# A two-layer hybrid backbone: the experts' activations kept in PSUM, and the gates' two parts summed by TensorE

## The chip, the cores and the metric

The kernel runs on one core of one Trainium2 chip. The metric is the device time of one execution in microseconds: three runs of the kernel before took 4037.82, 4032.03 and 4036.75 us, median 4036.75.

## The reference

Two layers over 256 latent and 256 context tokens of width 1024. Layer 0 mixes by a short gated convolution beside grouped attention, layer 1 by a bidirectional RWKV-7 recurrence. After the mixer of each layer stands a PEER expert network; the change is inside it:

```
def chunk_fn(xc):
    q = (xc @ w_q).reshape(n, PEER_HEADS, 2, PEER_HALF)
    s = jnp.einsum('nhpd,hpkd->nhpk', q, sub_keys)
    s1, i1 = lax.top_k(s[:, :, 0], PEER_TOPK)
    s2, i2 = lax.top_k(s[:, :, 1], PEER_TOPK)
    ...
    top_s, pos = lax.top_k(cand_s, PEER_TOPK)
    idx = jnp.take_along_axis(cand_i, pos, axis=-1)
    gate = jax.nn.softmax(top_s, axis=-1)
    act = jax.nn.gelu(jnp.einsum('nd,nhkd->nhk', xc, u_tab[idx]), approximate=False)
    return jnp.einsum('nhk,nhkd->nd', gate * act, v_tab[idx])
```

There are 128 x 128 = 16384 experts of one neuron each. Every token takes 16 of them for each of 8 heads.

## The kernel before

The kernel doesn't gather experts. It computes all 16384 activations for 256 tokens densely, 128 experts at a time, and multiplies them by a gate matrix that is zero for experts not chosen. One such group of 128 experts is called an expert tile here, numbered E. There are three passes of 128 tiles: the context tokens of layer 0 (E 0 to 127), its latent tokens (E 128 to 255), both in one `Peer` object, and, in a second object after layer 1's mixer, the latent tokens of layer 1.

Float32 precision comes from splits: a value is cast to `fp32r` on ScalarE (`S.copy` in `split`, L1175) and the remainder is subtracted on VectorE or GpSimd (L1176). A product of two split operands is three TensorE products (`mm3`, L1180 to L1182).

For each tile, `Peer.run` issues:

- `first(E)`: 24 products of 128 x 256 into `H`, a bank of PSUM, then Gelu on ScalarE into `W` in SBUF (L1056);
- `gate(E)`: VectorE multiplies `W` by the gates `G` of that tile into `W2` in SBUF (L1062), ScalarE casts it to `gwh`, VectorE subtracts to get `gwl`;
- every second tile, `gen(gq, j)`: the gates of 16 tokens for the quarter `gq` of 32 tiles that comes next. VectorE builds one-hot matrices `oh`, `eq` and `A` (a high and a low part of the gate) in fp16, TensorE multiplies them (L1007) into two PSUM tiles with both parts side by side, ScalarE copies the high part into `G` (L1011) and VectorE adds the low part (L1012). Only for quarter 0 of each object does TensorE accumulate both parts in one tile (L1000), which ScalarE copies whole (L1001);
- `last(E - 1)`: the second product of the tile before, 12 products of 128 x 512 (L1077) into four PSUM accumulators `acc`, then the split of the next `v` (cast on ScalarE, subtraction on GpSimd) and its load on the SP queue;
- the split of the next `u` (the subtraction half on VectorE, half on GpSimd, L1037) and its load.

Tiles 0 to 31 of each object (`LOOK`) have `first` done beforehand, while the experts are still being chosen, and keep their 32 results `W0` to `W31` in SBUF; in the loop they run only gate and second product.

From tile 32 to 255 the first object carries other work between its own, the shadow: choosing the experts of the latent tokens (to tile 92), layer 1's modulation (93 to 124) and layer 1's recurrence over the context tokens (132 to 253; 8 groups of two heads, 4 scan steps each). `beside` hands it out: each tile has four slots, and a task moves on when the units done fall behind a straight line from its start to its end. The tile planner then fixes each engine's order at compile time.

PSUM has eight banks, four for tiles tagged `acc`, which the accumulators of a pass occupy, and four for those tagged `mm`: `H`, the gates' tiles `p` and all products of the shadow take these in turn. In a scan step they are `rhs` (L469, L473), `pu` (L478) and `pS` (L488).

Of the kernel before, what the change touches and what calls it, by code (L numbers as in the profile page):

```python
# [7 lines left out]
F32 = mybir.dt.float32  # L8
# [4 lines left out]
AF = mybir.ActivationFunctionType  # L13
# [48 lines left out]
NSEL, NADA, NCTX = 68.0 + 16 * WKEYS + 16 * WPAIR, 30.0, 326.0 + 69 * WPROJ  # L62
TSEL, TCTX = 92, 132
LOOK = 32
WB = 4
GSCALE = 32768.0


# [122 lines left out]
def do(gen):  # L191

    while True:
        try:
            next(gen)
        except StopIteration as e:
            return e.value
# [22 lines left out]
def beside(work, at):  # L220


    done, slot = [0.0] * len(work), [at]

    def shadow(E):
        at = slot[0]
        slot[0] += 1
        for i, (t0, t1, n, gen) in enumerate(work):
            due = n * (at - 4 * t0) / (4 * (t1 - t0))
            while at > 4 * t0 and (done[i] < due or at >= 4 * t1):  # L230
                try:
                    done[i] += took(next(gen))
                except StopIteration:
                    break

    return shadow
# [588 lines left out]
class Peer:  # L825
# [6 lines left out]
    def __init__(self, k, keep, passes, shadow=None, h=None):  # L832
        self.k, self.keep, self.passes, self.shadow, self.h = k, keep, passes, shadow, h
        self.NT = 128 * len(passes)
        self.XS, self.IT, self.ACC, self.GT, self.U, self.V, self.W = {}, {}, {}, {}, {}, {}, {}
        self.es = ExitStack()
# [135 lines left out]
    def gen(self, gq, j):  # L972

        n, q = divmod(gq, 4)
        pl, V = self.pl, self.k.V
        i16, g16 = self.IT[n]
        if j == 0:
            self.GT[gq] = self.pg[gq % 2].tile([128, 32, 256], F32, name="G")
        s = slice(16 * j, 16 * j + 16)

        def per_token(t):

            return t[:, s].rearrange("p (t u) -> p t u", u=2)[:, :, None, :]


        oh = self.po.tile([128, 8, 128, 2], F16, name="oh")
        V.tensor_tensor(oh, self.iotaR[:, None].to_broadcast([128, 8, 128, 2]), per_token(i16[:, 1]).to_broadcast([128, 8, 128, 2]), ALU.is_equal)  # L987
        sh = [128, 8, 32, 2]
        A = pl.tile([128, 2, 8, 32, 2], F16, name="A", bufs=1)
        eq = pl.tile([128, 8, 32, 2], F16, name="eq", bufs=1)  # L990
        V.tensor_tensor(eq, self.iotaR[:, None, 32 * q:32 * q + 32].to_broadcast(sh), per_token(i16[:, 0]).to_broadcast(sh), ALU.is_equal)
        for i in range(2):
            V.tensor_tensor(A[:, i], eq, per_token(g16[:, i]).to_broadcast(sh), ALU.mult)  # L993
        G = self.GT[gq]
        if gq == 0:
            p = self.k.acc()
            for m in range(16):
                t, u = divmod(m, 2)
                for i in range(2):
                    self.k.T.matmul(p[:, 32 * m:32 * m + 32], lhsT=oh[:, t, :, u], rhs=A[:, i, t, :, u], start=i == 0, stop=i == 1)  # L1000
            self.k.S.copy(G[:, :, s].rearrange("p e n -> p n e"), p.rearrange("p (n e) -> p n e", n=16))  # L1001
            return
        for h in range(2):
            p = self.k.mm()
            for m in range(8):
                t, u = divmod(8 * h + m, 2)
                self.k.T.matmul(p[:, 64 * m:64 * m + 64], lhsT=oh[:, t, :, u], rhs=A[:, :, t, :, u], start=True, stop=True)  # L1007
            t = 16 * j + 8 * h
            p4 = p.rearrange("p (n i e) -> p n i e", n=8, i=2)
            g = G[:, :, t:t + 8].rearrange("p e n -> p n e")  # L1010
            self.k.S.copy(g, p4[:, :, 0])  # L1011
            V.tensor_tensor(g, g, p4[:, :, 1], ALU.add)  # L1012
# [33 lines left out]

    def first(self, E, slot=lambda: None):
        n = E // 128
        H = self.k.mm()
        u, x = self.U.pop(E), self.XS[n]  # L1050
        for t in range(8):
            self.k.mm3(H[:, :256], (u[0][:, t], u[1][:, t]), (x[0][:, t], x[1][:, t]), t == 0, t == 7)
            if t == 3:
                slot()
        W = self.pw.tile([128, 256], F32, name=f"W{E}") if E < LOOK else self.pl.tile([128, 256], F32, name="W", bufs=WB)
        self.k.S.activation(W, H[:, :256], AF.Gelu)  # L1056
        self.W[E] = W

    def gate(self, E):
        pl = self.pl  # L1060
        W2 = pl.tile([128, 256], F32, name="W2", bufs=1)
        self.k.V.tensor_mul(W2, self.W[E], self.GT[E // 32][:, E % 32])  # L1062
        wh = pl.tile([128, 256], F32R, name="gwh", bufs=2)
        wl = pl.tile([128, 256], F32R, name="gwl", bufs=2)
        self.k.split(wh, wl, W2)
        self.W[E] = (wh, wl)

    def second(self, E, slot=lambda: None):
        n, e = divmod(E, 128)
        if e == 0:  # L1070
            self.ACC[n] = [self.k.acc(name=f"acc{i}") for i in range(4)]
        wh, wl = self.W.pop(E)
        vh, vl = self.V.pop(E)
# [65 lines left out]
class K:  # L1139
# [454 lines left out]
    def out_proj(self, ws, pl, ch, cl, gate, h):  # L1594

        for g in range(4):
            wh, wl = next(ws)
            gt = self.gate_cols(pl, gate[0], 2, gate[1], 256 * g, 256)
            for b in range(2):
                p = self.mm()  # L1600
                s = slice(128 * b, 128 * b + 128)
                for k in range(8):
                    self.mm3(p[:, :256], (ch[:, k, s], cl[:, k, s]), (wh[:, k], wl[:, k]), k == 0, k == 7)
                y = pl.tile([128, 256], F32, name="yproj", bufs=2)
                cs = slice(256 * g, 256 * g + 256)
                self.V.tensor_mul(y, p[:, :256], gt)
                self.P.tensor_tensor(h[:, b, cs], h[:, b, cs], y, ALU.add)
            yield
# [591 lines left out]
```

## Time and profile before

| | |
|---|---|
| median of three runs | 4036.75 us (4032.03 to 4037.82) |
| the profiled execution | 4039.33 us, span 4037.5 us, mean granted clock 0.925 |
| busy, share of the span | PE 87%, DVE 77%, POOL 50%, ACT 43% |
| on the chain that ended last | PE 32%, DVE 18%, issue 3%, POOL 2%, ACT 1% of the span |

Busy is the time in which an engine worked; PE is TensorE, DVE is VectorE, ACT is ScalarE, POOL is GpSimd, and PEld is TensorE's loading of weights beside its products. The chain is followed back from the last instruction to what released each; the shares of the chain add up to 56%, as it reaches back to 1736 us only. The two `Peer` loops lie at 490 to 2630 us and 3325 to 4030 us of the span.

### The profile page before, as it was taken

Reading aid. Unit: us, or ns where it says so; the run is one execution under the profiler, and the core shown is the slowest. Engines: PE = TensorE matmul, PEld = TensorE weight load, DVE = VectorE, ACT = ScalarE, POOL = GpSimd, SP = SyncE. Lnnn points to the kernel's source line nnn. Section 1 sums busy time; section 2 is a strip of 40 time slices with the busy share of each in tenths; the row PEclk is TensorE's granted clock in tenths of the full one; section 3 lists DMA queues with packets and bytes.
Section 4 is the critical chain, followed back from the end, with each engine's and each line's share of the span. In section 5 each row is a group of like instructions: output and inputs, shape, how many; then the busy total and the mean of one; then the engine's idle time right before and its main releaser. Section 6 shows DMA issues by size and latency. Waiting matters only on the chain.

```text
span 4037.5 us, 69764 instructions
## 1 busy us (share of the span) xinstructions
PE 3528.5 (87%) x27239; PEld 3038.3 (75%) x27239; DVE 3115.6 (77%) x5626; ACT 1734.0 (43%) x2929; POOL 2024.0 (50%) x1126
## 2 busy tenths in 40 slices
PE   7998878997899989988888889987778787999999
PEld 6687757986778878866677677776666775898898
DVE  3559898779976788687777776577786979999944
ACT  3343444544444444544343343343313344455544
POOL 2022545654556555644444444544435353577776
PEclk9999899998999989988898999987788899999999
DMA  7462345654478745543333333451014234555565
GB/s 231 130 226 90 105 126 167 190 175 126 132 243 262 234 138 168 168 121 101 100 111 106 101 128 114 136 157 52 22 49 137 74 116 125 156 177 174 178 189 156
DMA packets 298644, 574.23 MB, mean 142 GB/s; under 512 B 36901, under 2 KB 193449, under 8 KB 297289
## 3 DMA queue, kind: packets, MB, share of 16 engines
q1 hardware_dynamic: 298312, 569.77, 45.8%
q8 instruction: 213, 3.49, 0.4%
q14 instruction: 119, 0.97, 0.1%
HBM read 555.51 MB, written 14.19 MB: 141 GB/s over the span
## 4 chain that ended last, share of the span: by engine, by line
PE 32%; DVE 18%; issue 3%; POOL 2%; ACT 1%; DMA 0%; DVEq 0%; POOLq 0%; ACTq 0%
PE acc L1077 11%; PE mm L1180 5%; PE mm L1181 5%; PE mm L1182 5%; DVE prod L437 2%; DVE gwl L1176 2%; DVE TT L440 2%; DVE A L993 1%; DVE oh L987 1%; DVE ul L1037 1%; PE mm L806 1%; DVE G L1012 1%; PE mm L669 1%; DVE t L661 1%; PE mm L1007 1%
## 5 line engine op out<-in xcount | busy, mean ns | idle before, releaser
L1176 POOL TENSOR_TENSOR vl<-raw,vh 128x1024 fp32r<-128x1024 f32 x352 | 912.3, 2592 | 755.5 <-ACT vh L1175 631.5
L1037 POOL TENSOR_TENSOR ul<-raw,uh 128x512 fp32r<-128x512 f32 x448 | 714.6, 1602 | 548.1 <-ACT uh L1034 499.1
L1180 PE MATMUL mm<-xh,uh 128*128 128x256 f32 x3072 | 905.8, 295 | 25.2 <-ACT uh L1034 24.4
L1181 PE MATMUL mm<-xh,ul 128*128 128x256 f32 x3072 | 896.2, 292 | 7.6 <-POOL ul L1037 3.9
L1182 PE MATMUL mm<-xl,uh 128*128 128x256 f32 x3072 | 890.6, 290 | 0.0
L1180 PEld LDWEIGHTS mm<-xh,uh 128*128 128x128 f32 x3072 | 609.4, 198 | 50.4 <-ACT uh L1034 25.2
L1181 PEld LDWEIGHTS mm<-xh,ul 128*128 128x128 f32 x3072 | 610.1, 199 | 22.6 <-POOL ul L1037 6.7
L1182 PEld LDWEIGHTS mm<-xl,uh 128*128 128x128 f32 x3072 | 609.7, 198 | 19.6 <-issue 18.2
L1077 PE MATMUL acc<-vh,gwh 128*128 128x512 f32 x1536 | 530.9, 427 | 98.6 <-ACT gwh L1175 98.1
L1077 PE MATMUL acc<-vh,gwl 128*128 128x512 f32 x1536 | 520.2, 420 | 77.9 <-DVE gwl L1176 77.5
L1062 DVE TENSOR_TENSOR W<-W,G 128x256 f32<-128x256 f32 x384 | 312.8, 815 | 356.5 <-ACT W L1056 354.9
L1077 PE MATMUL acc<-vl,gwh 128*128 128x512 f32 x1536 | 507.7, 412 | 0.8 <-DVE vl L1176 0.8
L1175 ACT CAST vh<-raw 128x1024 fp32r<-128x1024 f32 x384 | 404.0, 1052 | 143.8 <-issue 70.5
L1077 PEld LDWEIGHTS acc<-vh,gwl 128*128 128x128 f32 x1536 | 294.9, 199 | 183.8 <-DVE gwl L1176 125.6
L1175 ACT CAST gwh<-W 128x256 fp32r<-128x256 f32 x384 | 155.9, 406 | 640.4 <-DVE W L1062 569.5
L1034 ACT CAST uh<-raw 128x1024 fp32r<-128x1024 f32 x384 | 400.5, 1043 | 35.0 <-DMA raw<-in_peer_u_dram 34.8
L1077 PEld LDWEIGHTS acc<-vh,gwh 128*128 128x128 f32 x1536 | 274.2, 199 | 160.0 <-ACT gwh L1175 114.8
L1056 ACT ACTIVATE W<-mm 128x256 f32<-128x256 f32 x384 | 147.1, 383 | 499.1 <-PE mm L1182 496.3
L1077 PEld LDWEIGHTS acc<-vl,gwh 128*128 128x128 f32 x1536 | 304.0, 199 | 73.6 <-DVE vl L1176 1.7
L987 DVE TENSOR_TENSOR oh<-iotaR,i 128x2048 f16<-128x2048 f16 x192 | 336.1, 1751 | 20.7 <-ACT i L902 20.6
L1176 DVE TENSOR_TENSOR gwl<-W,gwh 128x256 fp32r<-128x256 f32 x384 | 328.1, 855 | 10.7 <-ACT gwh L1175 10.2
L1037 DVE TENSOR_TENSOR ul<-raw,uh 128x512 fp32r<-128x512 f32 x320 | 272.2, 851 | 44.2 <-ACT uh L1034 40.4
(418 smaller groups left out, 6297.9 us busy)
## 6 DMA issues: line engine op xcount, KB each, us to landing
raw<-in_peer_u_dram SPq DMA_DIRECT2D x384, 512.0 KB, 3.7
raw<-in_peer_v_dram SPq DMA_DIRECT2D x384, 512.0 KB, 3.7
wraw<-in_ada_w_dram SPq DMA_DIRECT2D x48, 1024.0 KB, 6.7
wraw<-in_peer_wq_dram SPq DMA_DIRECT2D x16, 1024.0 KB, 9.0
wraw<-in_ev_w_in_dram SPq DMA_DIRECT2D x9, 1024.0 KB
wraw<-in_ev_w_out_dram SPq DMA_DIRECT2D x8, 1024.0 KB, 8.1
wraw<-in_peer_wq_dram SPq DMA_DIRECT2D x16, 512.0 KB
wraw<-in_od_w_k_dram SPq DMA_DIRECT2D x8, 512.0 KB, 5.5
```

Of the source, the lines that this page charges most:

```text
L437: e.tensor_tensor(pv, TT[:, :, 0:c, t, None].to_broadcast(sh), L[:, t + 1:, :, t].rearrange("p t g -> p g t")[:, :, None, :].to_broadcast( ...
L987: V.tensor_tensor(oh, self.iotaR[:, None].to_broadcast([128, 8, 128, 2]), per_token(i16[:, 1]).to_broadcast([128, 8, 128, 2]), ALU.is_equal)
L1034: k.S.copy(uh, ur)
L1037: (le or (k.V, k.P)[i]).tensor_sub(ul[:, t], ur[:, t], uh[:, t].bitcast(F32))
L1056: self.k.S.activation(W, H[:, :256], AF.Gelu)
L1062: self.k.V.tensor_mul(W2, self.W[E], self.GT[E // 32][:, E % 32])
L1077: self.k.T.matmul(self.ACC[n][2 * tb + dh], lhsT=a[:, 128 * tb:128 * tb + 128], rhs=b[:, 512 * dh:512 * dh + 512], start=e == 0 and a is w ...
L1175: self.last_copy = self.S.copy(hi, src).ins
L1176: (le or self.V).tensor_sub(lo, src, hi.bitcast(F32))
L1180: self.T.matmul(out, lhsT=ah, rhs=bh, start=start, stop=False)
L1181: self.T.matmul(out, lhsT=al, rhs=bh, start=False, stop=False)
L1182: self.T.matmul(out, lhsT=ah, rhs=bl, start=False, stop=stop)
```

## The change

The list of buffers for `W` goes. In `first`, the result of tiles from 32 on is no longer copied to SBUF: Gelu writes it back into its own PSUM bank `H`. In `gate` the product with the gates is written into the same bank, or, for the first 32 tiles, whose `W` is still in SBUF, into a fresh `mm` bank. The split reads from there. In `gen`, the accumulating form that only quarter 0 had is used in all quarters of the object that has a shadow (the first two passes), in an `mm` bank but for quarter 0; the third pass keeps the two tiles and the additions for its quarters 1 to 3.

```
@@ gen
-        if gq == 0:
-            p = self.k.acc()
+        if gq == 0 or self.shadow:
+            p = self.k.mm() if gq else self.k.acc()
             for m in range(16):
                 t, u = divmod(m, 2)
                 for i in range(2):
                     self.k.T.matmul(p[:, 32 * m:32 * m + 32], lhsT=oh[:, t, :, u], rhs=A[:, i, t, :, u], start=i == 0, stop=i == 1)
             self.k.S.copy(G[:, :, s].rearrange("p e n -> p n e"), p.rearrange("p (n e) -> p n e", n=16))
             return
@@ first
-        H = self.k.mm()
+        H = self.k.mm()[:, :256]
...
-        W = self.pw.tile([128, 256], F32, name=f"W{E}") if E < LOOK else self.pl.tile([128, 256], F32, name="W", bufs=WB)
-        self.k.S.activation(W, H[:, :256], AF.Gelu)
+        W = self.pw.tile([128, 256], F32, name=f"W{E}") if E < LOOK else H
+        self.k.S.activation(W, H, AF.Gelu)
@@ gate
-        W2 = pl.tile([128, 256], F32, name="W2", bufs=1)
-        self.k.V.tensor_mul(W2, self.W[E], self.GT[E // 32][:, E % 32])
+        W = self.W[E]
+        W2 = self.k.mm()[:, :256] if E < LOOK else W
+        self.k.V.tensor_mul(W2, W, self.GT[E // 32][:, E % 32])
         wh = pl.tile([128, 256], F32R, name="gwh", bufs=2)
         wl = pl.tile([128, 256], F32R, name="gwl", bufs=2)
         self.k.split(wh, wl, W2)
```

## Rows read from the trace of the kernel before

**Rows 1.** Busy time by stage: stretch, length, engines, clock, DMA share, GB/s.

```profile
490.00:640.00 150.00, 118.72 (x772) 89.08 (x771) 141.62 (x189) 67.17 (x107) 65.89 (x23) 0.94 0.42 128
640.00:1127.00 487.00, 439.00 (x3101) 391.55 (x3100) 418.49 (x927) 228.16 (x360) 276.10 (x132) 0.95 0.53 160
1127.00:1423.00 296.00, 282.00 (x2188) 233.54 (x2187) 212.39 (x278) 140.72 (x235) 173.41 (x82) 0.97 0.76 249
1423.00:2630.00 1207.00, 1050.18 (x7951) 886.47 (x7950) 899.77 (x1445) 506.13 (x901) 603.35 (x347) 0.91 0.41 123
3325.00:3468.00 143.00, 113.32 (x666) 85.08 (x665) 134.84 (x180) 62.07 (x100) 55.24 (x19) 0.92 0.40 125
3468.00:4030.00 562.00, 562.00 (x3958) 506.47 (x3956) 431.21 (x474) 283.55 (x445) 406.86 (x191) 1.00 0.58 176
```

**Rows 2.** Groups by line: busy us, mean ns of one, idle before and releasers.

```profile
L1176 DVE TENSOR_TENSOR gwl<-W,gwh 128x256 fp32r<-128x256 f32 x384 | 328.1, 855 | 10.7 <-ACT gwh L1175 10.2
L1062 DVE TENSOR_TENSOR W<-W,G 128x256 f32<-128x256 f32 x384 | 312.8, 815 | 356.5 <-ACT W L1056 354.9
```

**Rows 3.** Single instructions, by tile and by line: ns least/median/most, first and last start.

```profile
L1062 DVE TENSOR_TENSOR W<-W,G x384: 354/425/2608, 499.5 to 4025.2; 128x256 f32<-128x256 f32 x192
...
L1176 DVE TENSOR_TENSOR gwl<-W,gwh x384: 373/420/3552, 502.5 to 4026.1; 128x256 fp32r<-128x256 f32 x192
...
L682 DVE TENSOR_TENSOR R<-mm,r x24: 677/691/692, 1801.8 to 2553.7; 128x512 f32<-128x512 f32 x24
...
L1037 DVE TENSOR_TENSOR ul<-raw,uh x320: 650/684/2887, 503.7 to 4014.8; 128x512 fp32r<-128x512 f32 x160
```

**Rows 4.** Timeline at 3520 and 3527 us: start us, duration us, engine, line, operation.

```profile
3520.59 2.60 POOL L1176 TENSOR_TENSOR vl<-raw,vh 128x1024 fp32r<-128x1024 f32 x1 [1.22 <-DVE ul L1037]
...
3520.84 1.35 DVE L1012 TENSOR_TENSOR G<-G,mm 128x256 f32<-128x256 f32 x2
...
3527.51 2.40 POOL L1176 TENSOR_TENSOR vl<-raw,vh 128x1024 fp32r<-128x1024 f32 x1 [2.08 <-ACT vh L1175]
...
3527.74 2.45 DVE L1062 TENSOR_TENSOR W<-W,G 128x256 f32<-128x256 f32 x1 [0.76 <-ACT W L1056]
```

**Rows 5.** Timeline of VectorE, one round of two tiles among the first 32.

```profile
549.75 1.37 DVE L1012 TENSOR_TENSOR G<-G,mm 128x256 f32<-128x256 f32 x2
...
558.31 1.36 DVE L1012 TENSOR_TENSOR G<-G,mm 128x256 f32<-128x256 f32 x2
```

**Rows 6.** Timeline of TensorE: the accumulating burst of quarter 0, and the other.

```profile
3257.46 0.97 PE L1000 MATMUL acc<-A,oh 128*128 128x32 f16 x32
...
3527.10 0.66 PE L1007 MATMUL mm<-A,oh 128*128 128x64 f16 x16
```

**Rows 7.** Waits of TensorE in 490 to 2630: us in total, times, longest.

```profile
PE acc L1077 <- ACT gwh L1175: 94.1, 54, 4.7
PE acc L1077 <- DVE gwl L1176: 58.2, 55, 4.9
```

**Rows 8.** The chain of waits in 1736 to 2630, by line, shares of the stretch.

```profile
by line: PE acc L1077 13.1%; PE mm L1180 7.2%; PE mm L1182 6.2%; PE mm L1181 6.1%; DVE prod L437 5.7%; DVE TT L440 5.5%; DVE gwl L1176 4.9%; DVE ul L1037 4.4%; issue 4.2%; DVE oh L987 3.4%; PE mm L669 3.4%; DVE G L1012 2.9%; DVE t L661 2.7%
```

**Rows 9.** Timelines of TensorE, ScalarE and VectorE around one scan step.

```profile
2060.01 0.39 PE L1180 MATMUL mm<-xh,uh 128*128 128x256 f32 x1
...
2064.43 0.33 PE L478 MATMUL mm<-rsb,R 64*64 64x64 f32 x4
...
2066.56 0.66 PE L1007 MATMUL mm<-A,oh 128*128 128x64 f16 x16
...
2068.61 0.45 PE L488 MATMUL mm<-UV,tok 128*64 128x64 f32 x6
...
2070.14 0.39 PE L1180 MATMUL mm<-xh,uh 128*128 128x256 f32 x1
...
2067.61 0.39 ACT L1056 ACTIVATE W<-mm 128x256 f32<-128x256 f32 x1
...
2071.13 3.55 DVE L1176 TENSOR_TENSOR gwl<-W,gwh 128x256 fp32r<-128x256 f32 x1
```

More of the change, by code (lines that the diff above doesn't have):

```diff
@@ L64 @@
 LOOK = 32
-WB = 4
 GSCALE = 32768.0
@@ L1048, in first @@
         n = E // 128
-        H = self.k.mm()
+        H = self.k.mm()[:, :256]
         u, x = self.U.pop(E), self.XS[n]
         for t in range(8):
-            self.k.mm3(H[:, :256], (u[0][:, t], u[1][:, t]), (x[0][:, t], x[1][:, t]), t == 0, t == 7)
+            self.k.mm3(H, (u[0][:, t], u[1][:, t]), (x[0][:, t], x[1][:, t]), t == 0, t == 7)
             if t == 3:
                 slot()
-        W = self.pw.tile([128, 256], F32, name=f"W{E}") if E < LOOK else self.pl.tile([128, 256], F32, name="W", bufs=WB)
-        self.k.S.activation(W, H[:, :256], AF.Gelu)
+        W = self.pw.tile([128, 256], F32, name=f"W{E}") if E < LOOK else H
+        self.k.S.activation(W, H, AF.Gelu)
         self.W[E] = W
```

## The prediction

> **What bounds the kernel now.** I read the busy times by stage first, then the chain of waits, then what TensorE waits for, then single instructions. By stage [rows 1] the reader sees three regimes. The last 562 us (third pass from expert 32 on) have TensorE busy for all of it at granted clock 1.00: nothing done on VectorE can help there. The two stretches of 150 and 143 us in which experts 0 to 31 are only summed (their first product was made earlier) are VectorE's: 141.62 and 134.84 us busy, TensorE 118.72 and 113.32. Between them, 640 to 2630, both are near their limit: TensorE 90% busy in 640 to 1127, 95% in 1127 to 1423, 87% in 1423 to 2630, at clocks from 0.91 to 0.97, VectorE 72 to 86%. The chain of 1736 to 2630 [rows 8] mixes TensorE's products with VectorE's lines, so of a microsecond taken from either, the other gives part back. TensorE waits in 490 to 2630 most for the gate's two results, 94.1 and 58.2 us [rows 7].
>
> VectorE's lines are long for a reason that the rows show. The gate's product takes 425 ns in the median but 815 in the mean and 2608 at most, `gwl` 420, 855 and 3552 [rows 2, 3]. At 3527.74 the product starts 0.23 us after a GpSimd subtraction of 2.40 us and ends 0.28 us after it; at 3520.84 two additions that read one operand from PSUM run through under a GpSimd subtraction, 1.35 us for both [rows 4]. So a VectorE operation with both inputs in SBUF is held by a running GpSimd one, and one with a PSUM input is not.
>
> **The change part by part.** The sums are made against the profiled execution, 4039.33 us (span 4037.5 and 1.83 around it); it lies 2.58 us above the median 4036.75, and the forecast is carried over to the median.
>
> *Additions of the low part.* The gates of the second to eighth quarter (7 x 16 = 112 calls) lose two VectorE additions each, 1.35 to 1.37 us a pair [rows 4, 5]. Sixteen of them lie in 490 to 640: there one round of two experts lasts 549.75 to 558.31, 8.56 us, filled by VectorE [rows 5]. 16 x 1.35 = 21.6; I take -20, since TensorE follows at 118.72/150 of 8.56, 6.8 us a round. Of the other 96 calls, 30 lie in 640 to 1127, 20 in 1127 to 1423, 46 in 1423 to 2630 (none after expert 223). The chain gives the additions 2.9% of 894 us = 26 us [rows 8], where 32 calls last 43 us: 60% on the path. 76 x 1.35 x 0.6 = 61; the 20 calls beside a TensorE at 95% I count as nothing. Half of the 61 stays, because TensorE is late next: -30 (ends 0 and -61).
>
> *The gate's operations are held less.* From expert 32 on the product reads PSUM and SBUF, and `gwl` too in all passes; before expert 32 the product still reads two SBUF tiles. The excess is 815 - 425 = 390 and 855 - 420 = 435 ns each. On the chain `gwl` has 4.9% of 894 = 44 us [rows 8], of it 435/855 = 51%, 22 us; for the other 800 us of shadowed work (487, and 1423 to 1736) in proportion 20. The first rounds of passes one and three add little, their product stays held. The wait then meets the next operation with two SBUF inputs (`oh` or `A`), so I keep 60%: -25 (ends 0 and -42). In the last 562 us it is worth 0: TensorE hides it.
>
> *Cost of PSUM operands on VectorE and ScalarE.* VectorE's reading: 691 ns for 512 elements from PSUM against 684 from SBUF [rows 3], so 0. [...] VectorE writing to PSUM, and ScalarE writing it in place, the trace does not show. Between 354 ns (the fastest product) and 691 (twice the elements) [rows 3] I take the median 425, being the nearest row, hence no cost; the upper end is 266 ns x 256 = 68 us of VectorE, half on the path, +34. ScalarE reads the same 256 columns from PSUM in 0.39 us already [rows 9]; the cast from there I cost at nothing, ScalarE, 42 to 48% busy in these stages [rows 1], covering it. The one wide ScalarE copy of the gates replaces two half ones over the same elements, also nothing.
>
> *TensorE's accumulation.* 16 products of 64 columns become 32 of 32. The trace has both: 0.66 us a burst, and 0.97 [rows 6]; +0.31 x 112 = 35 us. In the first 16 VectorE hides them. The 20 calls in 1127 to 1423 count whole, 6; of the other 76 (24 us) half: +18 in all (ends +6 and +30). Nothing new waits for POOL, SP or a transfer; no DMA is moved.
>
> *PSUM banks held longer.* `H` was free after Gelu; it now stays until `gwl`. At one scan step: first product of `H` 2060.01, Gelu done at 2068.0, `gwl` done at 2074.68 [rows 9], so 8.0 us become 14.7. There are four `mm` banks; behind `H` come the scan's `pu`, the gates' `p` and the scan's `pS` [rows 9], and the next expert's `H` (2070.14) is the fifth: it would wait 4.5 us, or, if `gwl` is no longer held (2071.13 + 0.42), 1.4. Behind it on TensorE stand its 24 products, the rest of the scan step and the second product, and the scan's chain waits for those. Such steps number 8 x 4 = 32: 45 to 144 us of TensorE time. In 640 to 1423 fewer products of the shadowed work lie between, and the one `p` instead of two eases it; in the third pass only `p`, `p` and one `H` lie between: 0. I take the low price and a third of it on the path: +15 (ends 0 and +144).
>
> *Clock.* Fewer gate waits leave TensorE less idle; it runs at 0.91 to 0.97 where it waits and at 1.00 where it doesn't [rows 1]. One part in a hundred of 1990 us is 20; I take -12 (ends 0 and -40).
>
> Sum: -20 - 30 - 25 + 0 + 18 + 15 - 12 = -54. 4039.33 - 54 = 3985.3; at the median 4036.75 - 54 = 3983. The instructions' order on each engine is fixed at compile time and is not that of the source (`A` of a call runs beside another expert's gate), so all of it will be laid anew; my ends are wide for that.
>
> **The rivals.**
>
> *A. VectorE was the whole limit.* What is late next is not TensorE but nothing: the additions give 20 + 61, the port 42, the clock 40, TensorE costs 18: -145, 3892. For it: the gate waits of 152 us [rows 7] and VectorE at 94% in the first stage. Against: TensorE 87 to 95% busy between.
>
> *B. TensorE takes all of it back.* Between 640 and 2630 the relief ends at TensorE, which has 35 us more to do: -20 - 25 + 35 + 15 = +5, 4042. For it: 95% in 1127 to 1423. Against: 13% idle in 1423 to 2630.
>
> *C. The held banks serialize the scan (slower).* If each of the 32 scan steps waits the full 4.5 us on the path, +144 against -69 of the other terms: +75, 4112. It decides from 69/32 = 2.2 us a step. For it: `gwl` comes 7 us after Gelu in the rows, because VectorE is behind. Against: 1.4 us once `gwl` isn't held. [...]
>
> *D. PSUM operands cost VectorE more than the rows at 512 elements.* [...]
>
> **How the numbers follow.** Less than 0.2% (8 us) cannot be told from no change. Forecast 0.48, its own range 3930 to 4025; A 0.14; D 0.06; B 0.11; C 0.21. Faster: 0.48 + 0.14 + 0.06 = 0.68. Same 0.10, slower 0.22 (B's upper part and C). The range 3895 to 4065 leaves out the better half of A (0.07) and the greater part of C (0.13).
>
> **What would show it.** Right: the additions gone from 490 to 2630; `gwl`'s mean near 0.45 us in all passes, the product's too but in the first 32 experts; 112 bursts of 0.97 us; a first stage shorter by 20 us; the last 562 us unchanged; less waiting for `gwh` and `gwl`. Wrong: products on `mm` that wait for `gwl` or Gelu by several microseconds each in 1423 to 2630 (C); a `gwl` or product of 0.5 us and more without a GpSimd operation beside it (D); a TensorE at 95% and no shorter stage (B). The forecast is wrong as a whole if 1423 to 2630 becomes longer.

## The result, and the profile after

The kernel after takes 3930.82 us (median of four runs, 3927.68 to 3938.05) against 4035.93 for the kernel before: ratio 0.9743, 95% interval 0.9726 to 0.976. The forecast was 3983, the range 3895 to 4065. The direction and the main mechanism held; the gain, 105 us, is about twice the 54 us forecast.

Busy time by stage of the kernel after (stretch, length, then PE, PEld, DVE, ACT, POOL, granted clock, DMA share, GB/s):

```profile
496.00:640.00 144.00, 132.47 (x1137) 108.50 (x1136) 130.70 (x175) 77.22 (x109) 67.11 (x31) 0.95 0.47 153
640.00:1110.00 470.00, 431.55 (x3551) 391.05 (x3546) 350.93 (x858) 222.93 (x323) 260.90 (x128) 0.95 0.53 168
1110.00:1405.00 295.00, 284.71 (x2499) 238.41 (x2496) 167.10 (x240) 137.86 (x212) 164.79 (x84) 0.98 0.72 243
1405.00:2547.00 1142.00, 1030.36 (x8604) 877.96 (x8602) 771.84 (x1340) 495.18 (x846) 598.79 (x342) 0.93 0.41 129
3235.00:3372.00 137.00, 116.44 (x708) 88.99 (x707) 129.04 (x187) 63.14 (x104) 50.23 (x21) 0.94 0.41 139
3372.00:3925.00 553.00, 552.80 (x3908) 502.88 (x3906) 259.63 (x468) 280.08 (x439) 419.72 (x189) 1.00 0.55 176
```

Neither these stretches nor those of [rows 1] are cut exactly at the tiles they stand for (their bounds lie up to 18 us off), so their lengths can't be compared row by row. Cut at the same tiles, the long stretch (tiles 132 to 255) went from 1193 to 1142 us; TensorE is busy 90% of it, where it was 87%, and VectorE fell from 74% to 68%. In the last row TensorE is still busy throughout, and the stretch is hardly shorter.

The groups by line (busy us, mean ns of one, idle before and its releasers):

```profile
L1176 DVE TENSOR_TENSOR gwl<-mm,gwh 128x256 fp32r<-128x256 f32 x384 | 159.2, 415 | 5.6 <-ACT gwh L1175 5.4
L1062 DVE TENSOR_TENSOR mm<-mm,G 128x256 f32<-128x256 f32 x320 | 137.1, 429 | 609.9 <-ACT mm L1055 609.2
L1062 DVE TENSOR_TENSOR mm<-W,G 128x256 f32<-128x256 f32 x64 | 46.0, 742 | 0.0
L1011 DVE TENSOR_TENSOR G<-G,mm 128x256 f32<-128x256 f32 x96 | 64.5, 717 | 0.2
```

and the same by single instructions (ns least/median/most, first and last start):

```profile
L1176 DVE TENSOR_TENSOR gwl<-mm,gwh x384: 401/416/425, 511.4 to 3920.6; 128x256 fp32r<-128x256 f32 x192
L1062 DVE TENSOR_TENSOR mm<-mm,G x320: 389/432/435, 622.9 to 3919.8; 128x256 f32<-128x256 f32 x160
L1062 DVE TENSOR_TENSOR mm<-W,G x64: 410/421/2636, 508.1 to 3356.8; 128x256 f32<-128x256 f32 x64
```

Read the maxima against [rows 3]: `gwl` had 3552 ns at most and now has 425, the product from PSUM 435. Only the products of the 64 tiles of passes one and three that still read `W` in SBUF reach 2636. Of the additions 96 are left, those of the third pass (224 additions are gone).

What TensorE waits for in 490 to 2547 (us in total, times, longest) answers to [rows 7]:

```profile
PE acc L1077 <- ACT gwh L1175: 80.8, 36, 5.9
PE acc L1077 <- DVE gwl L1176: 36.2, 34, 4.5
```

The waits for the gate's two results fell from 152 to 117 us. The chain of waits in 1650 to 2547, to be read against [rows 8]:

```profile
by line: PE acc L1077 20.1%; PE mm L1180 7.8%; PE mm L1182 7.0%; DVE prod L436 6.8%; PE mm L1181 6.8%; DVE TT L439 5.1%; issue 3.9%; PE mm L668 3.7%; DVE ul L1036 3.0%; PE mm L487 2.7%; DVE oh L986 2.0%; DVE t L660 1.8%; DVE A L992 1.8%; DV
```

TensorE's four lines have 41.7% of it (32.6% before); `gwl`, 4.9% before, and the additions `G`, 2.9%, are no longer among the lines shown, which end at 1.8%. Lines of the scan (`prod`, `TT`) have stayed.

The first stage, on VectorE (start us, duration us, engine, line), answers to [rows 5]:

```profile
549.26 2.96 DVE L1062 TENSOR_TENSOR mm<-W,G 128x256 f32<-128x256 f32 x2
...
553.14 1.21 DVE L986 TENSOR_TENSOR oh<-iotaR,i 128x2048 f16<-128x2048 f16 x1
...
556.08 0.75 DVE L1062 TENSOR_TENSOR mm<-W,G 128x256 f32<-128x256 f32 x2
556.75 0.41 DVE L992 TENSOR_TENSOR A<-eq,g 128x512 f16<-128x512 f16 x1
557.09 0.41 DVE L1176 TENSOR_TENSOR gwl<-mm,gwh 128x256 fp32r<-128x256 f32 x1
557.42 2.29 DVE L992 TENSOR_TENSOR A<-eq,g 128x512 f16<-128x512 f16 x1
...
566.45 1.21 DVE L986 TENSOR_TENSOR oh<-iotaR,i 128x2048 f16<-128x2048 f16 x1
```

and on GpSimd:

```profile
549.37 2.56 POOL L1176 TENSOR_TENSOR vl<-raw,vh 128x1024 fp32r<-128x1024 f32 x1 [3.26 <-ACT vh L1175]
556.29 3.14 POOL L1176 TENSOR_TENSOR vl<-raw,vh 128x1024 fp32r<-128x1024 f32 x1 [4.35 <-ACT vh L1175]
```

While GpSimd subtracts from 556.29 to 559.43, `gwl` with its PSUM operand runs in 0.41 us at 557.09, and `A`, behind it, with two SBUF inputs, ends 0.28 us after GpSimd. Here the holding has moved to the next operation that can be held. Over the whole execution most of it went: `oh`, `eq`, `A` and VectorE's `ul`, which still read two SBUF tiles, took 1035 us together before and take 1020 now, while `gwl` and the products fell from 641 to 342. Counted one by one, all of the 140 `gwl` and 96 products that before took over 0.15 us more than the fastest quarter ran beside a GpSimd operation; after, 236 `gwl` ran beside GpSimd's subtraction of `vl` or `ul`, and none of them took more than 425 ns.

And VectorE runs ahead: two products stand side by side (`x2`); with one buffer for `W2` the second waited until `gwl` of the first was done. Two rounds last from 553.14 to 566.45, 6.65 us each, where one lasted 8.56 [rows 5].

**Where the 105 us are.** A stage runs here from the start of the first second product (L1077) of one tile to that of another (tiles 224-255 to the end of the last product of tile 255). Lengths of before and differences to it, in us, each from one profiled execution:

| tiles | before | after | e1 | e2 | e3 | e4 | e5 | e6 | e7 | e8 | e9 | e10 | e11 | e12 |
|---|---|---|---|---|---|---|---|---|---|---|---|---|---|---|
| ahead of tile 0 | 503.2 | +6.8 | +0.6 | +5.4 | +5.3 | +6.5 | +5.9 | +2.7 | +2.9 | +4.5 | +1.5 | +0.4 | +2.8 | +4.0 |
| pass 1, 0-31 | 153.2 | -30.9 | -19.6 | -17.8 | -12.2 | -29.9 | -30.8 | -17.9 | -31.9 | -30.6 | -1.9 | -32.3 | -26.7 | -29.8 |
| 32-91 | 487.3 | -9.6 | -10.8 | -4.0 | -1.2 | -11.7 | -6.7 | -9.6 | -11.8 | -12.8 | -2.5 | -46.5 | -10.6 | -12.9 |
| 92-131 | 297.4 | -2.0 | +3.6 | -7.5 | -0.8 | +0.5 | +2.4 | -0.9 | +2.0 | +0.8 | +0.5 | -14.9 | +1.6 | -2.4 |
| 132-159 | 257.5 | -8.9 | -3.3 | -3.3 | +0.9 | -9.4 | -9.7 | -5.0 | -7.0 | -6.0 | +6.3 | -30.1 | -4.3 | -11.3 |
| 160-223 | 669.7 | -36.0 | -31.2 | -35.5 | +2.8 | -35.2 | -35.7 | -26.7 | -38.7 | -43.4 | +9.5 | -90.7 | -27.2 | -47.7 |
| 224-255 | 265.3 | -6.1 | -1.3 | -6.7 | -1.5 | -6.1 | -6.0 | -1.7 | -2.8 | -11.5 | -4.7 | -18.6 | 0.0 | -12.1 |
| between the loops | 694.5 | -2.8 | -1.4 | +3.7 | -1.8 | +0.1 | -3.6 | +1.7 | -3.3 | +21.7 | +13.5 | -4.7 | -0.8 | +2.3 |
| pass 3, 0-31 | 146.0 | -12.5 | -1.7 | -14.1 | -7.4 | -31.5 | -31.2 | +5.6 | -12.8 | -12.4 | -3.1 | -33.7 | -10.1 | -30.7 |
| pass 3, 32-95 | 381.4 | -3.5 | +0.6 | -3.5 | -0.7 | -3.5 | +6.2 | -3.5 | +18.4 | -3.5 | +0.6 | -3.5 | 0.0 | -3.5 |

(e1 to e12 are the runs below.) After: -30.9 in the first stage, -62.6 in tiles 32 to 255, -16.0 in the third pass, +4.0 elsewhere, where only the instructions' order changed. The order alone can move a row by some 6 us: in tiles 0 to 31 of pass three e6 issues the same instructions as the kernel before, and has +5.6. The first two rows belong together, since the first stage gains in part what the stretch ahead of it loses: up to tile 32 the kernel after has gained 24.1 us, e1 19.0 and e3 6.9.

### The profile page after: what moved, and what is told of

Read it like the earlier page. It is cut to its first block, busy times and chain, and to the rows that moved or that the text cites. A ratio compares the mean times of both kernels' runs of the same rounds, so it can differ in the third digit from the quotient of the medians.

```text
span 3932.0 us, 73000 instructions
## 1 busy us (share of the span) xinstructions
PE 3513.2 (89%) x29031; PEld 3054.5 (78%) x29031; DVE 2681.8 (68%) x5402; ACT 1725.2 (44%) x2817; POOL 2003.1 (51%) x1126
## 4 chain that ended last, share of the span: by engine, by line
PE 44%; DVE 20%; issue 3%; POOL 2%; ACT 1%; DMA 0%; DVEq 0%; SPq 0%; POOLq 0%; ACTq 0%
PE acc L1077 16%; PE mm L1180 7%; PE mm L1182 7%; PE mm L1181 7%; DVE A L992 2%; DVE prod L436 2%; DVE TT L439 1%; DVE oh L986 1%; DVE ul L1036 1%; PE mm L805 1%; PE mm L668 1%; PE mm L999 1%; DVE mm L1062 1%; DVE eq L990 1%; PE mm L1290 1%
## 5 line engine op out<-in xcount | busy, mean ns | idle before, releaser
L1036 POOL TENSOR_TENSOR ul<-raw,uh 128x512 fp32r<-128x512 f32 x448 | 691.8, 1551 | 637.1 <-ACT uh L1033 599.0
L1181 PEld LDWEIGHTS mm<-xh,ul 128*128 128x128 f32 x3072 | 605.5, 197 | 17.9 <-POOL ul L1036 6.2
L1077 PE MATMUL acc<-vh,gwh 128*128 128x512 f32 x1536 | 524.2, 423 | 83.4 <-ACT gwh L1175 83.4
L1062 DVE TENSOR_TENSOR mm<-mm,G 128x256 f32<-128x256 f32 x320 | 137.1, 429 | 609.9 <-ACT mm L1055 609.2
L1077 PE MATMUL acc<-vh,gwl 128*128 128x512 f32 x1536 | 509.3, 414 | 41.9 <-DVE gwl L1176 39.3
L1077 PE MATMUL acc<-vl,gwh 128*128 128x512 f32 x1536 | 501.2, 408 | 12.2 <-DVE vl L1176 11.8
L1033 ACT CAST uh<-raw 128x1024 fp32r<-128x1024 f32 x384 | 399.5, 1041 | 13.6 <-DMA raw<-in_peer_u_dram 13.3
L1077 PEld LDWEIGHTS acc<-vh,gwl 128*128 128x128 f32 x1536 | 297.8, 198 | 132.2 <-DVE gwl L1176 67.1
L1077 PEld LDWEIGHTS acc<-vh,gwh 128*128 128x128 f32 x1536 | 271.7, 197 | 135.5 <-ACT gwh L1175 90.9
L1077 PEld LDWEIGHTS acc<-vl,gwh 128*128 128x128 f32 x1536 | 300.4, 197 | 84.0 <-DVE vl L1176 15.1
L1036 DVE TENSOR_TENSOR ul<-raw,uh 128x512 fp32r<-128x512 f32 x320 | 310.1, 969 | 72.2 <-ACT uh L1033 68.4
L1055 ACT ACTIVATE mm<-mm 128x256 f32<-128x256 f32 x320 | 118.2, 369 | 544.0 <-PE mm L1182 543.3
L986 DVE TENSOR_TENSOR oh<-iotaR,i 128x2048 f16<-128x2048 f16 x192 | 272.6, 1420 | 21.8 <-ACT i L901 21.7
L992 DVE TENSOR_TENSOR A<-eq,g 128x512 f16<-128x512 f16 x384 | 251.2, 685 | 28.9 <-PE acc L999 23.7
L1175 ACT CAST gwh<-mm 128x256 fp32r<-128x256 f32 x384 | 142.9, 372 | 268.4 <-DVE mm L1062 268.3
```

Source lines behind the costliest of these rows:

```text
L1033: k.S.copy(uh, ur)
L1036: (le or (k.V, k.P)[i]).tensor_sub(ul[:, t], ur[:, t], uh[:, t].bitcast(F32))
L1055: self.k.S.activation(W, H, AF.Gelu)
L1062: self.k.V.tensor_mul(W2, W, self.GT[E // 32][:, E % 32])
L1077: self.k.T.matmul(self.ACC[n][2 * tb + dh], lhsT=a[:, 128 * tb:128 * tb + 128], rhs=b[:, 512 * dh:512 * dh + 512], start=e == 0 and a is w ...
L1175: self.last_copy = self.S.copy(hi, src).ins
```

## The experiments

Times are medians of four to six runs; each ratio is to the kernel before on the same chip, and gains in us are worked out from the ratios, times 4036.

### The two halves of the change

**e1**, the kernel before with the accumulation alone:

```
-        if gq == 0:
-            p = self.k.acc()
+        if gq == 0 or self.shadow:
+            p = self.k.mm() if gq else self.k.acc()
```

> The kernel before with only the gates' accumulation on TensorE in the first two passes; the activations go through SBUF as before. Theory P (the prediction's: the additions' time leaves VectorE, the gate's operations are no longer held by GpSimd, the two gains add up to the 105 us measured): 3975 to 3995, that is 40 to 60 us less than before; of it 18 to 24 in tiles 0 to 31 of the first pass; the means of the gate's product and of gwl stay near 815 and 855 ns. Rival R (what helped is that the weighted activations have four banks in place of one SBUF buffer, so that VectorE runs ahead): at most 25 us less, 4010 or more. Rival S (half of the change costs: TensorE's longer bursts eat the additions' gain): 4025 to 4045.

3980.32 us, ratio 0.9861 (0.9846 to 0.9876): 56 us less, in the range of P. `gwl` and the product stay held:

```profile
L1062 DVE TENSOR_TENSOR W<-W,G 128x256 f32<-128x256 f32 x384 | 325.5, 848 | 392.5 <-ACT W L1056 390.5
L1176 DVE TENSOR_TENSOR gwl<-W,gwh 128x256 fp32r<-128x256 f32 x384 | 315.1, 820 | 8.5 <-ACT gwh L1175 8.0
```

**e2**, the kernel after with the additions put back on VectorE, so that only the activations' place in PSUM is left of the change:

```
-        if gq == 0 or self.shadow:
-            p = self.k.mm() if gq else self.k.acc()
+        if gq == 0:
+            p = self.k.acc()
```

> The changed kernel with the gates summed by VectorE again in quarters 1 to 7 of the first two passes; activations in PSUM. P: 3975 to 3995; the means of gwl and of the product from tile 32 on near 0.43 us; tiles 0 to 31 of the third pass as in the changed kernel, 12 us shorter than before; this gain and that of the other half add up to 105 within 15 us. R: 3940 to 3955, nearly the whole. S: 3930 or less, below the changed kernel.

3961.56 us, 0.9818 (0.9802 to 0.9835): 73 us less, with `gwl` at

```profile
L1176 DVE TENSOR_TENSOR gwl<-mm,gwh 128x256 fp32r<-128x256 f32 x384 | 159.5, 415 | 5.1 <-ACT gwh L1175 4.9
```

The time lies between the ranges of P and R. Each half brings more alone than the forecast gave to both, and they don't add up within the 15 us that P allowed: 56 + 73 is 129, the whole brings 104. One stage alone overlaps by as much: in tiles 160 to 223 e1 has -31.2, e2 -35.5 and both together -36.0. Either relief is enough there.

### Which part of the move into PSUM

**e6**, the kernel after with the product from PSUM written to one SBUF buffer, as before:

```
-        W2 = self.k.mm()[:, :256] if E < LOOK else W
+        W2 = pl.tile([128, 256], F32, name="W2", bufs=1)
```

> The changed kernel, but the weighted activations W2 go to the one SBUF buffer as before: the product reads PSUM (and frees the bank when it ends), gwl reads two SBUF tiles. P: the product's mean from tile 32 on near 0.43 us, gwl's near 0.85; about half of the activations' gain is gone: 20 to 30 us slower than the changed kernel, 3950 to 3960. R: as good as all of the activations' gain is gone, 3975 to 3995. If the held bank costs (rival C of the prediction), freeing it at the product gives something back: 3935 or less.

3977.01 us, 0.9848 (0.9834 to 0.9861).

```profile
L1176 DVE TENSOR_TENSOR gwl<-W,gwh 128x256 fp32r<-128x256 f32 x384 | 368.9, 961 | 9.7 <-ACT gwh L1175 9.2
L1062 DVE TENSOR_TENSOR W<-mm,G 128x256 f32<-128x256 f32 x320 | 134.1, 419 | 464.2 <-ACT mm L1055 463.4
```

The product is free and `gwl` takes the holding. The two means are those of P, the time is that of R: all of the activations' gain is gone (e1, without it, has 0.9861). The run takes back two things at once, the free `gwl` and the further buffers; e3, e7 and e11 tell them apart. Its profiled execution is 49 us longer than that of the kernel after; 31 of them lie in the two stages of tiles 0 to 31 (13.0 and 18.1) and 18 in 132 to 255. The timeline of VectorE in the first stage shows a round without additions and with one buffer:

```profile
549.28 1.22 DVE L986 TENSOR_TENSOR oh<-iotaR,i 128x2048 f16<-128x2048 f16 x1
...
552.34 2.50 DVE L1062 TENSOR_TENSOR W<-W,G 128x256 f32<-128x256 f32 x1
...
555.39 0.43 DVE L1176 TENSOR_TENSOR gwl<-W,gwh 128x256 fp32r<-128x256 f32 x1 [0.21 <-ACT gwh L1175]
...
556.40 1.22 DVE L986 TENSOR_TENSOR oh<-iotaR,i 128x2048 f16<-128x2048 f16 x1
```

7.12 us a round, 1.44 below before's 8.56; the banks take off another 0.47 (6.65). With one buffer the second product can't be made before `gwl` of the first is, so the next `gwl` waits for a fresh `gwh` each round. Sixteen times 0.47 is 7.5 of the 13.0 us by which this stage is longer than after; nearly all the rest is its first round, 14.8 us where the kernel after has 8.6.

**e7**, the other way round: Gelu writes to SBUF as before, the product always goes to a fresh bank, and `gwl` reads PSUM:

```
-        W = self.pw.tile(...) if E < LOOK else H
+        W = self.pw.tile(...) if E < LOOK else self.pl.tile([128, 256], F32, name="W", bufs=4)
-        W2 = self.k.mm()[:, :256] if E < LOOK else W
+        W2 = self.k.mm()[:, :256]
```

> The changed kernel, but Gelu writes to SBUF (four buffers) and the product, from two SBUF tiles, writes a fresh PSUM bank, which is held from the product to gwl only. P: the product's mean near 0.8 us, gwl's near 0.42; 20 to 30 us slower than the changed kernel, 3950 to 3960. R: within 8 us of the changed kernel, as W2 has its four banks. Rival C of the prediction: 3925 or less, as the bank is held a shorter time.

3953.86 us, 0.9791 (0.9771 to 0.9812). The product is held again, `gwl` is not:

```profile
L1062 DVE TENSOR_TENSOR mm<-W,G 128x256 f32<-128x256 f32 x384 | 293.2, 767 | 490.1 <-ACT W L1055 489.3
L1176 DVE TENSOR_TENSOR gwl<-mm,gwh 128x256 fp32r<-128x256 f32 x384 | 159.1, 415 | 7.1 <-ACT gwh L1175 6.6
```

In the first two passes it has all the gain (-90.2 from tile 0 to 255; after: -93.5). So a held product costs nothing there; the free `gwl` and the fresh buffer are what pays. The time is that which P expected, but not for P's reason. Its loss is in tiles 32 to 95 of pass three, +18.4, where TensorE, elsewhere busy throughout, has short waits (3371 to 3771):

```profile
PE acc L1077 <- ACT gwh L1175: 13.0, 25, 0.8
```

The kernel before has a held product in that stage too, and no such loss; why a fresh bank turns it into a wait is not settled.

**e3**, the kernel before with four buffers for `W2`:

```
-        W2 = pl.tile([128, 256], F32, name="W2", bufs=1)
+        W2 = pl.tile([128, 256], F32, name="W2", bufs=4)
```

> The kernel before with four SBUF buffers in place of one for the weighted activations W2, nothing else. R (VectorE's running ahead is the activations' gain): 3960 to 3985, and in tiles 0 to 31 of the third pass about 12 us less. P (gwl being held by GpSimd is what went): gwl's mean stays near 0.85 us, 4025 to 4040; at most 10 us in tiles 0 to 31 of the passes, where VectorE stands 0.21 us a round for the cast.

4017.73 us, 0.9951 (0.9938 to 0.9964): 20 us less, with `gwl` at 821 and the product at 833 ns, held as before. Neither range holds it. The table has -12.2 and -7.4 in the two stages of tiles 0 to 31, +5.3 ahead of the first, and no more than 3 us in any other row: running ahead by itself, a gain that the prediction has no term for.

**e11**, e1 and e3 together:

```
-        if gq == 0:
-            p = self.k.acc()
+        if gq == 0 or self.shadow:
+            p = self.k.mm() if gq else self.k.acc()
...
-        W2 = pl.tile([128, 256], F32, name="W2", bufs=1)
+        W2 = pl.tile([128, 256], F32, name="W2", bufs=4)
```

> The kernel before with TensorE's accumulation of the gates and four SBUF buffers for the weighted activations: run-ahead as in the changed kernel, but gwl and the product are held by GpSimd as before. R (run-ahead is what is left of the activations' gain beside the accumulation, 50 us in the runs so far: 3980 against 3931): 3930 to 3945. P (being held is): 3970 to 3980. Both, with run-ahead's 20 us in tiles 0 to 31 of passes one and three as its run by itself showed: 3955 to 3965.

3962.41 us, 0.9807 (0.9793 to 0.982), in the range for both. That makes a chain from before to after, in ratios: the accumulation takes it to 0.9861 (-56 us), running ahead to 0.9807 (-22), operations that are no longer held to 0.9743 (-26). Each step is uncertain by some 8 us.

e7 and e11 differ only in where `W2` lies, in a bank or in one of four SBUF buffers, so that `gwl` takes 415 ns in e7 and 800 in e11. From tile 0 to 255 e7 has -90.2 and e11 -67.2: 23.0 us are the price of the held `gwl` there, 11.5 of them in tiles 160 to 223.

The shares depend on the order in which they are taken. The other way round, running ahead brings 20 us (e3), the free operations 54 more (e3 to e2), and the accumulation, taken last, 30 (e2 to after).

### What the accumulation costs TensorE

**e4**, the kernel after, with the additions of the third pass's second quarter (made in its tiles 0 to 31) also on TensorE:

```
-        if gq == 0 or self.shadow:
+        if gq < 2 or self.shadow:
```

> The changed kernel with TensorE's accumulation also in quarter 1 of the third pass, whose gates are made in its tiles 0 to 31 (16 calls). P: VectorE fills those rounds, so 16 x 1.3 = 20 us go there as in the first pass: 10 to 20 us less than the changed kernel, 3911 to 3922, all of it before tile 32 of that pass. S: TensorE's longer bursts take it back, 3925 to 3935.

3915.4 us, 0.9691 (0.967 to 0.9711): 21 us better than after, as P has it. Tiles 0 to 31 of pass three take 114.6 us instead of 133.5. In the kernel after VectorE is busy for 129.04 of 137 us there and TensorE for 116.44, in e4 (3243 to 3357) for 111.21 and 111.57 of 114.

**e5**, all quarters:

```
-        if gq == 0 or self.shadow:
+        if True:
```

> The changed kernel with TensorE's accumulation in all quarters of the third pass (48 calls). From tile 32 on TensorE is busy all the time there. P: quarter 1 gains as in the run before; quarters 2 and 3 cost 32 x 0.31 = 10 us by the bursts' lengths, or 32 x 0.45 = 14 by the distance of their starts: within 5 us of the changed kernel, and 10 to 14 us slower than with quarter 1 alone, all in tiles 32 to 95 of that pass. S: more than 20 us slower than with quarter 1 alone.

3922.41 us, 0.9715 (0.97 to 0.9731): 8 us below the kernel after, where P allowed 5, and 10 above e4 by the ratios. Against e4 it differs in 32 calls in tiles 32 to 95 of pass three, where TensorE is busy throughout. That stage, e4's and then e5's:

```profile
3357.00:3735.00 378.00, 378.00 (x2803) 344.61 (x2803) 217.21 (x374) 200.95 (x318) 292.65 (x129) 1.00 0.55 178
```

```profile
3357.00:3745.00 388.00, 388.00 (x3301) 354.93 (x3301) 253.57 (x312) 199.72 (x287) 262.14 (x129) 1.00 0.53 174
```

9.7 us by the stage's own bounds, 0.30 a call: the 0.31 of [rows 6], paid in full.

### The banks held longer

**e8** and **e9**, the kernel after and the kernel before with three banks for `mm` instead of four:

```
-        return self.ps.tile(list(shape), F32, name=name, tag="mm")
+        return self.ps.tile(list(shape), F32, name=name, tag="mm", bufs=3)
```

> The changed kernel with three PSUM banks in place of four for the tiles tagged mm (shadow and third pass alike). If held banks cost (rival C of the prediction), one bank less hurts the changed kernel more than the kernel before: over 40 us more than the changed kernel, and more than 20 us above what the kernel before loses by the same cut. If they are as good as free (the trace of the changed kernel shows no wait of TensorE for gwl before a product into mm), both lose about the same, 5 to 30 us: 3936 to 3960.

> The kernel before with the same three banks. Held banks cost: 4040 to 4055, a loss of at most 20 us, as Gelu frees H early. Free: a loss like the changed kernel's, 4042 to 4066.

e8: 3950.29 us, 0.978 (0.9767 to 0.9793), 15 us over the kernel after; e9: 4060.93, 1.0059 (1.0045 to 1.0073), 24 over before. Both are in the ranges for free banks. One bank less costs the kernel that holds them longer no more than the other, and e8 loses it outside the expert loops (+21.7 between them against -2.8); in tiles 0 to 255 it is no slower than after (-103.5 against -93.5).

The two runs differ in more than how long `H` is held: the kernel before also takes two banks `p` for each `gen` and keeps them until the additions, the kernel after takes one. e2, which holds `H` as the kernel after does and still has two `p`, shows what that is worth (its waits of TensorE, 490 to 2640):

```profile
PE mm L1180 <- DVE gwl L1176: 10.3, 8, 2.6
```

Such a product needs nothing of `gwl` but a bank, and with three smaller lines of this kind (L1290, L1006, L668) the waits come to 13.6 us. The kernel after has none of them. So rival C's wait exists, near the +15 of the sum, and with one `p` in place of two it is gone; a scan held up in every step, which C needs, no run shows.

### The source of the holding

**e10**, the kernel before with GpSimd writing zeros into `vl` instead of subtracting; the low part of `v` is left out, but for the odd tiles 0 to 31:

```
-        self.k.split(vh, vl, vr, self.k.V if E < LOOK and E % 2 else self.k.P)
+        if E < LOOK and E % 2:
+            self.k.split(vh, vl, vr)
+        else:
+            self.k.S.copy(vh, vr)
+            self.k.P.memset(vl.bitcast(F32), 0.0)
```

> The kernel before, but GpSimd writes zeros into vl, reading nothing, in place of subtracting (tiles 0 to 31 keep VectorE's subtraction for odd tiles): v's low part is left out of the second product. P: with no reading of SBUF by GpSimd beside it but the ul half, the means of the product and of gwl fall from 0.82 and 0.86 us to 0.5 to 0.6, and the time to 3950 to 3990. If the holding has another cause (VectorE's own order, a wait counted in), the means stay above 0.75 and the time moves by what an earlier vl gives, less than 15 us.

3770.87 us, 0.9339 (0.9324 to 0.9355): 267 us less, where 50 to 90 were expected.

```profile
L1180 DVE TENSOR_TENSOR gwl<-W,gwh 128x256 fp32r<-128x256 f32 x384 | 390.2, 1016 | 15.0 <-ACT gwh L1179 14.8
L1048 POOL MEMSET vl<- 128x1024 f32 x352 | 335.5, 953 | 402.6 <-PE acc L1081 338.3 <-DVE wl L1180 38.7 <-issue 13.5
L987 DVE TENSOR_TENSOR oh<-iotaR,i 128x2048 f16<-128x2048 f16 x192 | 246.7, 1285 | 20.6 <-ACT i L902 20.6
L1066 DVE TENSOR_TENSOR W<-W,G 128x256 f32<-128x256 f32 x384 | 186.4, 485 | 465.0 <-ACT W L1060 463.5
```

The product is nearly free (485 ns for 815), but `gwl` got longer, 1016 for 855, where 0.5 to 0.6 us were expected of both. The timeline shows one case, VectorE first and then GpSimd:

```profile
2004.78 1.50 DVE L1180 TENSOR_TENSOR gwl<-W,gwh 128x256 fp32r<-128x256 f32 x1
```

```profile
2004.14 1.86 POOL L1037 TENSOR_TENSOR ul<-raw,uh 128x512 fp32r<-128x512 f32 x1 [1.84 <-ACT uh L1034]
```

GpSimd's other subtraction, `ul`, now runs under it; of the 212 `gwl` that are long in this run 208 overlap one, 120 of 140 did before. So `ul` goes on holding VectorE, and the 267 us are an upper bound only for what `vl` does to it: the zeros also free GpSimd (its `vl` takes 335.5 us, 912.3 before) and make `vl` ready without waiting for `vh`, and this run doesn't tell these apart.

**e12**, e4 with GpSimd's subtraction cut in two:

```
...
+            for i in range(2):
+                c = slice(512 * i, 512 * i + 512)
+                self.k.P.tensor_sub(vl[:, c], vr[:, c], vh[:, c].bitcast(F32))
```

> The changed kernel with TensorE's accumulation also in quarter 1 of the third pass (3915), and GpSimd's subtraction of vl in two halves of 512 columns. P: a VectorE operation with two SBUF inputs is held for at most one half, 1.2 to 1.5 us in place of 2.4; oh, eq, A and ul together are still held some 340 us in the changed kernel, and about a third of that goes; with VectorE on half of the path: 3870 to 3900. Rival: the fixed time of one GpSimd instruction more, and a later end of vl, as it now waits for VectorE twice: 3915 to 3935.

3894.62 us, 0.965 (0.9636 to 0.9663): the fastest version that computes the reference, 17 us better than e4 (uncertain by some 10), in the range of P, and 38 better than after. Its halves, and `A` and `eq` on VectorE:

```profile
L1049 POOL TENSOR_TENSOR vl<-raw,vh 128x512 fp32r<-128x512 f32 x704 | 991.0, 1428 | 569.7 <-ACT vh L1046 444.2 <-PE mm L999 80.5 <-DVE ul L1036 13.6
...
L992 DVE TENSOR_TENSOR A<-eq,g 128x512 f16<-128x512 f16 x384 | 256.5, 699 | 22.3 <-PE acc L999 20.2 <-PE mm L999 0.8
L990 DVE TENSOR_TENSOR eq<-iotaR,i 128x512 f16<-128x512 f16 x192 | 161.8, 843 | 0.4
```

And its products from SBUF, by single instructions:

```profile
L1068 DVE TENSOR_TENSOR mm<-W,G x64: 415/421/1530, 505.3 to 3318.9; 128x256 f32<-128x256 f32 x64
```

GpSimd works longer for it (991 us against 914), but a product is held 1530 ns at most, not 2634. `A` was 728 and `eq` 906 ns in e4. The first stages gain nothing over e4 (-29.8 and -29.9; -30.7 and -31.5): there the second half holds the next operation instead (`A` behind the products takes 1.51 us at 542.17, the one behind the next `gwl` 0.41). The gain lies in tiles 160 to 255, -12.5 and -6.0 more than e4, the second no more than the order alone can do. Whether the shorter holding alone makes it, or also the first half that is ready earlier, stays open.

## Why the prediction was right, and its size wrong

The direction and the two reliefs were right, the sum was half of the gain, and the measured 3930.82 us lies at the very end of the forecast's own range, 3930 to 4025. That it lies inside at all is luck: the sum was 52 us off, and the range reached 53 below it.

**The additions.** In the first stage the forecast was -20 and e1, which has only this, measures -19.6. For the other calls the forecast was -30, with +18 for TensorE: -12. e1 measures -43.0 from tile 32 to 255. The step that failed is "half of the 61 stays, because TensorE is late next": it is not late next where most of the gain is, tiles 160 to 223 with the scan (-31.2). TensorE had 13% idle in the stretch around it [rows 1] and has 10% now. Where it was at 95%, tiles 92 to 131, the count of nothing held (+3.6). But e1 measures the accumulation taken first. Taken last it brings 30 us, near the forecast's 32 (20 + 30 - 18): in tiles 160 to 223 either relief finds the same idle time, and the sum had no such overlap in it.

**TensorE's price.** 0.31 us a call was right; e5 shows 0.30 where nothing hides it.

**The gate's operations.** -25 was forecast. e11 to after, -26, is this step with the accumulation in place, so in that order its size was right; without the accumulation it brings 54. What failed in any order is the sentence "the first rounds of passes one and three add little, their product stays held". It does stay held, but the new banks replace a single buffer, and VectorE runs ahead: 20 us in all in e3, 22 on top of the accumulation in e11. In the diff this is one word, `bufs=1`, that disappeared; I followed which operands changed their place and not how many there are of them. In the first stage 1.44 us of a steady round go with the additions and 0.47 with the further buffers; up to tile 32 the forecast had 20 us, and 19.0 came in e1, 24.1 in all; in pass three it had 0, and 16.0 came.

That "the wait then meets the next operation with two SBUF inputs" is seen at 557.42; in sum it is not, as `oh`, `eq`, `A` and `ul` take 1045 us in e1 and 1020 after, so nothing here bears out the 40% taken off for it. With one input in PSUM the 384 `gwl` of the kernel after never exceed 425 ns.

**PSUM operands (rival D).** 0 was right. From PSUM the product has 432 ns in the median, from SBUF 421, and `gwl` 416 where it had 420 [rows 3]; Gelu in place takes 369 ns on average. Rival D, with the +34 at 266 ns an instruction, would have shown 0.5 us and more; these medians differ by 11 ns at most.

**Banks (rival C).** +15 should have been 0. In the kernel after a single product waits for the gate's operations to give up a bank, 1.8 us for the cast. Not because they come sooner: from the end of Gelu to the end of `gwl` it is 4.0 us in the median of tiles 160 to 223, where it was 4.6, and up to 9.7. What e2, with its 13.6 us of such waits, has and the kernel after hasn't is the second `p`, kept until the additions; the prediction names this easing for 640 to 1423 only.

**Clock.** -12 was taken; the granted clock rose by 0.02 in the long stretch (0.91 to 0.93) and in pass three's first, by 0.01 in two others. Which part of the gain it is no run isolates.

**Rivals A and B.** B (TensorE takes it back) is wrong: every stage below TensorE's limit got shorter. A forecast 3892; the measured 3931 is 39 us from that and 52 from the forecast, nearer to the rival that was given 0.14. The 42 us that A's sum calls the port are the upper end of what the holding might give back; no run shows a port, only that `gwl` and the product are held. But A's premise, that the gains simply add, fails at the overlap of e1 and e2 in tiles 160 to 223.

In numbers, forecast and measured: first stage -20 and -30.9 (run-ahead, some 7 of it at the cost of the stretch ahead); tiles 32 to 255 -34 and -62.6 (by e1 the additions are worth 31 more net of TensorE's price, and there is no bank wait, 15; some 17 of this is lost again, as the reliefs overlap); pass three 0 and -16.0 (run-ahead); elsewhere 0 and +4.0.

## What to carry to other kernels

Where an operation's maximum is far above its median, as with `gwl` and the product [rows 3], find what runs beside it before counting its mean as work, and see whether giving it a PSUM operand (`gwl`: 425 ns at most in the kernel after), or cutting the other operation in two (the product from SBUF: 1530 ns at most in e12, 2634 in e4), lets it through. When a diff moves a tile from one pool to another, count its buffers as well as its place: four in place of one, and nothing else, gave 20 us here (e3). Two reliefs of one stage need not add (tiles 160 to 223: -31.2 and -35.5, together -36.0): measure each alone and both together.

## What the runs showed of the hardware

- In the kernel after VectorE writes to PSUM and reads from it at nearly SBUF's price for 256 columns of float32: 432 ns in the median of 320 products from PSUM to PSUM, 421 from SBUF to PSUM, 416 in 384 `gwl` from PSUM to SBUF; before, all in SBUF, 425 and 420.
- GpSimd's subtractions cost this kernel time: -17 us with that of `vl` in halves, where `gwl` is already free (e12 against e4), at most -267 without it, with the gate's operations still in SBUF (see e10). With GpSimd writing zeros, which reads nothing, `oh` took 1285 ns on average for 1751 in the kernel before.
- Freeing one operation can hold another longer: with the product free `gwl` went to 961 ns in e6 (820 in e1), and with `gwl` free `A` went to 836 in e7 (711 in e11). With both free, in the kernel after, the others did not get longer in sum. What counts is whether the one that is held stands on the path: in tiles 0 to 255 the product does not (e7 against after, 3.3 us), `gwl` does (e11 against e7, 23.0).
